# State-space x tiles of a hybrid diffusion layer turned to token-major by VectorE's 32x32 blocks and a pass through DRAM instead of by TensorE, with a group's B tile projected last

## The chip, the core and the metric

The kernel runs on one core of one Trainium2 chip. Five engines with a queue each work side by side: TensorE (PE in the profile; its weight loads are PEld), VectorE (DVE), ScalarE (ACT), GpSimd (POOL) and SyncE (SP), which here does little but issue transfers. The engines share the on-chip memory SBUF, the matmuls write to PSUM, and 16 DMA engines move data between DRAM and SBUF. Each engine takes its instructions in order; an instruction that waits holds up everything behind it on its engine. The metric is device time in microseconds (us), as the median over runs.

## What is computed

One layer over 512 latent tokens and 256 context tokens of width 1024, all in float32: a modulated RMSNorm, one wide input projection that feeds a bidirectional state-space mixer (Mamba-2 SSD, 4 groups of 8 heads) and a windowed attention, a gated merge, and a convolutional feed-forward part. The change touches how the state-space mixer gets its inputs. Cut to that:

```python
def ssd_prepare(xbc_raw, dt_raw, conv_w, conv_b, dt_bias, a_log):
    xbc = jax.nn.silu(dwconv_centred(xbc_raw, conv_w, conv_b))        # along tokens, per channel
    xs = xbc[..., :D_SSD].reshape(Bsz, L, SSD_GROUPS, SSD_HPG, SSD_HEADDIM)    # x: 2048 channels
    bm = xbc[..., D_SSD:D_SSD + D_BC].reshape(Bsz, L, SSD_GROUPS, SSD_STATE)   # B: 4 x 128
    cm = xbc[..., D_SSD + D_BC:].reshape(Bsz, L, SSD_GROUPS, SSD_STATE)        # C: 4 x 128
    ...
def ssd_scan(xs, la, bm, cm, h0, with_output):
    states = jnp.einsum('bcsgn,bgrcs,bcsgrp->bcgrpn', bc, decay_to_end, xc)    # sums over tokens s
    ...
    y_diag = jnp.einsum('bgrcls,bcsgrp->bclgrp', scores, xc)                   # sums over tokens s
    y_off = jnp.einsum('bclgn,bcgrpn,bgrcl->bclgrp', cc, states[:, :-1], jnp.exp(cs))
```

The convolution runs along tokens for each channel, so it wants channels on the partitions. The two sums over tokens `s` want x with tokens on the partitions. So every x tile is turned once between the two. The context tokens go through the same steps and give the scan its first states.

## The kernel before

**Products.** A float32 product is made of three fast passes: `split` (L182) makes of each weight tile (128 x 1024, `wraw`) a high part `whi` on ScalarE (L183, a cast) and a low part `wlo` on VectorE (L184, a subtraction), and `gemm` (L231) adds high x high, high x low and low x high in PSUM (L237, L238, L240). A latent product (LAT, 512 tokens wide) is 24 matmuls, a context product (CTX, 256 wide) is 24 shorter ones. The weight stream is loaded by SyncE into three `wraw` buffers; `whi` and `wlo` have two each. `run` (L210) issues load and split of the next step's weights ahead of each step.

**Projection steps.** `proj_steps(g)` (L1422) makes the six steps of a head group g: a B tile (`b_fn`, LAT and CTX), a C tile (`c_fn`, LAT) and four x tiles (`x_fn`, LAT and CTX). Each product goes through `conv_silu` (L1394): a ScalarE pass from PSUM (L1390), two VectorE passes (L1391, L1392), a tanh on ScalarE (L1398) and a last VectorE pass (L1399) that writes the channel-major tile, `tc` for x.

**Turning.** The finished tile is put on the list `TURN`; `turn` (L1413) makes a 128x128 TensorE transpose of each block of it into a PSUM bank (L1418: four for latent, two for context) and ScalarE copies the bank to its place in `xs` or `xsc` (L1462; L1439 for B). The transposes are emitted between the matmuls of a later product, by the list `BETWEEN`, which `gemm` calls at every third k.

**Scan.** `ssd_steps(g)` (L1486) scans group g while the projections of group g+1 run. Its first part, `states`, weighs the context tiles (`xw<-xsc`, L1491), multiplies them with the context B tiles (L1520) and walks back over the chunks (L1503). Then for each chunk of 128 tokens `chunk_in` builds the decay tiles `E` (L1593 to L1602) and `chunk_out` multiplies the states with C (L1610), the x tile with `E` (L1618) and turns the result (L1631).

**Order.** The loop at L1654 strings these together: after group 0's six steps comes, for each g, the `states` step, one filler product ("filler" below: a z or a gate tile, LAT alone), then the six steps of the next group with one chunk of group g behind each from the second on; for the last group fillers stand in place of projections. Within that, the scheduler of the tile framework fixes the order of each engine's queue before the program runs, from its own estimate of when things are ready. `xsc` has one buffer, `xs`, `BT`, `Bk` two, PSUM's `acc` three and `mis` five.

Of the kernel before, what the change touches and what calls it, by code (L numbers as in the profile page):

```python
# [9 lines left out]
F32 = mybir.dt.float32  # L10
# [8 lines left out]
P = 128  # L19
D = 1024  # L20
L = 512
LC = 256
# [22 lines left out]
def tile_hybrid_layer(  # L45
# [31 lines left out]
    nc = tc.nc  # L77
    V, S, G, T = nc.vector, nc.scalar, nc.gpsimd, nc.tensor
# [28 lines left out]
    def accb():  # L107
        return bank("acc")
# [158 lines left out]
    dt_d = dpool.tile([64, L + LC], F32, name="dt_d")  # L267
    tt_d = dpool.tile([64, 4], F32, name="tt_d")
    x1_d = dpool.tile([L, D], F32, name="x1_d")
    g2_d = dpool.tile([D], F32, name="g2_d")  # L270

    def col(base, i):
# [1121 lines left out]
    def conv_silu(ps, n, i, o):  # L1394
        a = tmp("ta")
        conv_half(ps, n, V_CW, V_CB, i, 24, a)
        t = tmp("tb")
        S.activation(t[:, :n], a[:, :n], AF.Tanh)  # L1398
        V.scalar_tensor_tensor(o[:, :n], t[:, :n], 1.0, a[:, :n], ALU.add, ALU.mult)  # L1399
# [13 lines left out]
    def turn(n=None):  # L1413

        for t, n_, put in TURN[:n]:
            ps = misb()
            for c in range(n_):
                T.transpose(ps[:, c * P : (c + 1) * P], t[:, c * P : (c + 1) * P], ident)  # L1418
            put(ps)
        del TURN[:n]  # L1420

    def proj_steps(g):  # L1422
        d = GR[g]

        def b_fn(w):
            d["xs"] = bp.tile([P, 4, 512], F32, tag="xs", name="xs", bufs=2)
            d["xsc"] = bp.tile([P, 2, 512], F32, tag="xsc", name="xsc", bufs=1)
            d["Bkc"] = bp.tile([P, 2, P], F32, tag="Bkc", name="Bkc", bufs=2)
            d["Bk"] = bp.tile([P, 4, P], F32, tag="Bk", name="Bk", bufs=2)
            d["BT"] = bp.tile([P, L], F32, tag="BT", name="BT", bufs=2)  # L1430
            pl, pc = accb(), accb()
            gemm([LAT(pl)], w)
            turn()
            gemm([CTX(pc)], w)
            conv_silu(pl, L, 16 + g, d["BT"])
            BTc = tmp("tc")
            conv_silu(pc, LC, 16 + g, BTc)
            for t, n, k in ((d["BT"], 4, d["Bk"]), (BTc, 2, d["Bkc"])):
                TURN.append((t, n, lambda ps, n=n, k=k: S.copy(flat(k), ps[:, : n * P])))  # L1439

        def c_fn(w):
            d["CT"] = bp.tile([P, L], F32, tag="CT", name="CT", bufs=2)
            pl = accb()
            gemm([LAT(pl)], w)
            turn(1)
            conv_silu(pl, L, 20 + g, d["CT"])

        def x_fn(ct, w):
            i = 4 * g + ct
            pl, pc = accb(), accb()  # L1450
            gemm([LAT(pl)], w)
            if not BETWEEN:
                BETWEEN.extend([lambda: None, lambda: turn(1), turn])
            gemm([CTX(pc)], w)
            for pp, n, dst in ((pl, L, d["xs"]), (pc, LC, d["xsc"])):
                xl = tmp("tc")
                conv_silu(pp, n, i, xl)
                TURN.append(
                    (
                        xl,  # L1460
                        n // P,
                        lambda ps, n=n, dst=dst: S.copy(  # L1462
                            dst[:, :, ct * P : (ct + 1) * P], ps[:, :n].rearrange("p (a b) -> p a b", b=P)
                        ),
                    )
                )
# [811 lines left out]
```

## Time and profile before

| | us |
|---|---|
| three runs: median (lowest to highest) | 1220.63 (1220.55 to 1221.63) |
| the profiled execution, its own time | 1221.22 |
| span of its instructions in the trace | 1219.4 |
| TensorE busy within the span | 1211.3 |
| VectorE / ScalarE / GpSimd busy | 924.5 / 684.4 / 182.3 |
| projections and scan, from the first group's first product to the last chunk | about 366 to 715 |

The profile lists, for each group of instructions, the source line, the engine, output<-input by the program's names, the shape and the count. A timeline row begins with the start in us from the span's start and the duration; what stands in brackets is idle time of the engine just before and who ended it. The starts of successive matmuls tell what each costs TensorE; the durations printed beside them overlap. The granted TensorE clock was 0.999 of full speed.

### The profile page before, as it was taken

How to read it: one execution, taken by the hardware profiler on the slowest of the kernel's cores; microseconds unless marked ns; L12 is line 12 of the kernel's file. 1: busy time of each engine (PE TensorE's matmuls, PEld its weight loads, DVE VectorE, ACT ScalarE, POOL GpSimd, SP SyncE). 2: the span in 40 equal slices, each digit the busy share in tenths (PEclk: the TensorE clock that was granted, in tenths of full speed). 3: DMA queues.
4: the chain of work that ended last, by engine and by line, in shares of the span. 5: the costliest groups of instructions: out<-in, count | busy, mean ns of one | idle time of the engine just before them, and what ended most of it. 6: DMA issues, size and time to landing. Idle time of an engine off the chain costs nothing.

```text
span 1219.4 us, 17443 instructions
## 1 busy us (share of the span) xinstructions
PE 1211.3 (99%) x6320; PEld 995.9 (82%) x6320; DVE 924.5 (76%) x1491; ACT 684.4 (56%) x1271; POOL 182.3 (15%) x183
## 2 busy tenths in 40 slices
PE   9999999999999999999999999999999999999997
PEld 6798888888878877778787778888988888888886
DVE  5857888888564698697896867677687877778778
ACT  5657787788544457476575664223544343436653
POOL 0000121100000043262451632000200000000021
PEclk9999999999999999999999999999999999999999
DMA  9645889844756335357366568777265534336662
GB/s 368 260 138 184 160 242 260 171 149 126 176 160 162 111 117 164 128 125 203 97 159 204 155 209 281 217 248 240 51 162 147 179 115 139 112 122 228 194 182 96
DMA packets 121383, 211.55 MB, mean 173 GB/s; under 512 B 25672, under 2 KB 67728, under 8 KB 121296
## 3 DMA queue, kind: packets, MB, share of 16 engines
q1 hardware_dynamic: 110256, 187.09, 49.4%
q0 software_dynamic: 10752, 23.07, 8.5%
q8 instruction: 50, 0.82, 0.3%
q14 instruction: 37, 0.30, 0.1%
q10 hardware_dynamic: 288, 0.27, 0.1%
HBM read 185.68 MB, written 42.28 MB: 187 GB/s over the span
## 4 chain that ended last, share of the span: by engine, by line
PE 96%; DVE 1%; issue 1%; ACT 1%; DMA 1%; POOL 0%; SPq 0%; POOLq 0%; DVEq 0%; ACTq 0%
PE acc L237 20%; PE acc L240 20%; PE acc L238 20%; PE score L957 3%; PE po L1006 3%; PE pt L993 2%; PE mis L579 2%; PE mis L1610 2%; PE mis L1503 2%; PE mis L1618 1%; PE mis L2137 1%; PE mis L2138 1%; PE mis L2139 1%; PE acc L2137 1%; PE acc L2139 1%; PE acc L2138 1%
## 5 line engine op out<-in xcount | busy, mean ns | idle before, releaser
L183 ACT CAST whi<-wraw 128x1024 fp32r<-128x1024 f32 (+1 forms) x115 | 120.6, 1049 | 158.0 <-PE acc L238 109.5
L184 DVE TENSOR_TENSOR wlo<-wraw,whi 128x1024 fp32r<-128x1024 f32 (+1 forms) x115 | 144.6, 1258 | 68.7 <-ACT whi L183 65.0
L237 PE MATMUL acc<-hlh,whi 128*128 128x512 f32 x472 | 194.2, 411 | 0.0
L238 PE MATMUL acc<-hll,whi 128*128 128x512 f32 x472 | 185.0, 392 | 0.0
L240 PE MATMUL acc<-hlh,wlo 128*128 128x512 f32 x472 | 184.9, 392 | 0.0
L237 PE MATMUL acc<-mh,whi 128*128 128x512 f32 x368 | 143.6, 390 | 0.0
L238 PE MATMUL acc<-ml,whi 128*128 128x512 f32 x368 | 143.2, 389 | 0.0
L240 PE MATMUL acc<-mh,wlo 128*128 128x512 f32 x368 | 143.2, 389 | 0.0
L240 PEld LDWEIGHTS acc<-hlh,wlo 128*128 128x128 f32 x472 | 88.6, 188 | 19.5
L237 PEld LDWEIGHTS acc<-hlh,whi 128*128 128x128 f32 x472 | 88.8, 188 | 17.9 <-issue 3.1
L238 PEld LDWEIGHTS acc<-hll,whi 128*128 128x128 f32 x472 | 88.9, 188 | 17.4 <-issue 2.4
L237 PEld LDWEIGHTS acc<-mh,whi 128*128 128x128 f32 x368 | 69.1, 188 | 14.5
L238 PEld LDWEIGHTS acc<-ml,whi 128*128 128x128 f32 x368 | 69.1, 188 | 14.3
L240 PEld LDWEIGHTS acc<-mh,wlo 128*128 128x128 f32 x368 | 69.1, 188 | 14.2
L1391 DVE SCALAR_TENSOR_TENSOR ta<-acc,half,ta 128x511 f32<-128x511 f32 (+1 forms) x66 | 43.9, 666 | 26.3 <-ACT ta L1390 26.0
L966 DVE CUSTOM_DVE_ANT_0 p<-score,winm,nsink 128x512 f32<-128x512 f32 (+1 forms) x64 | 51.9, 811 | 15.3 <-PE score L957 13.8
L1390 ACT ACTIVATE ta<-acc,half 128x512 f32<-128x512 f32 (+1 forms) x66 | 46.9, 710 | 22.1 <-PE acc L240 20.8
L973 ACT ACTIVATE p<-p,mneg 128x512 f32<-128x512 f32 (+1 forms) x64 | 49.8, 778 | 15.4 <-DVE mneg L966 14.8
L237 PE MATMUL acc<-hch,whi 128*128 128x256 f32 x176 | 54.7, 311 | 0.0
L1505 POOL TENSOR_TENSOR st<-st,eT 128x512 f32<-128x512 f32 x24 | 29.8, 1243 | 165.3 <-ACT st L1522 151.9
L164 POOL DMA_DIRECT2D dsum<-wdn x24 | 25.4, 1144 | 193.0 <-DVE wlo L1090 171.7
L795 DVE SCALAR_TENSOR_TENSOR tm<-wraw,csil,tm 128x512 f32<-128x512 f32 x56 | 44.1, 787 | 13.1 <-DMA wraw<-wm 12.5
(440 smaller groups left out, 2998.2 us busy)
## 6 DMA issues: line engine op xcount, KB each, us to landing
wraw<-wup SPq DMA_DIRECT2D x44, 512.0 KB, 3.7
dsum<-wdn POOLq DMA_DIRECT2D x24, 704.0 KB, 8.5
fb<-cs_d SPq DMA_DIRECT2D x32, 512.0 KB, 6.5
wraw<-wm SPq DMA_DIRECT2D x32, 512.0 KB, 3.9
wraw<-wx SPq DMA_DIRECT2D x24, 512.0 KB, 3.5
wm<-wm SPq DMA_DIRECT2D x16, 512.0 KB, 8.1
wraw<-wz SPq DMA_DIRECT2D x16, 512.0 KB, 3.9
wraw<-wos SPq DMA_DIRECT2D x16, 512.0 KB, 4.8
```

The lines of the kernel that those rows point to most:

```text
L183: F["cast"] = S.copy(hi[:, :n], r[:, :n])
L184: return V.tensor_tensor(lo[:, :n], r[:, :n], raw(hi[:, :n]), ALU.subtract)
L237: T.matmul(ps, wh, xh[:, k0 + k, :], start=a, stop=False)
L238: T.matmul(ps, wh, xl[:, k0 + k, :], start=False, stop=False)
L240: T.matmul(ps, wl, xh[:, k0 + k, :], start=False, stop=b)
L795: V.scalar_tensor_tensor(acc, r[:, u * 512 : u * 512 + 512], sc, acc, ALU.mult, ALU.add)
L957: T.matmul(ps[:, o : o + len(z) * P], Q[h][:, b * P : (b + 1) * P], k[:, j, z[0] * P : (z[-1] + 1) * P], start=v == 0 and o % 512 in (0, P ...
L966: V.tensor_tensor_reduce(p[:, :w], d["ps"][i][:, o0 : o0 + w], m, op0=ALU.add, op1=ALU.min, scale=1.0, scalar=nsink[:, h : h + 1], accum_o ...
L973: S.activation(p, p, AF.Exp, bias=d["mneg"][:, i : i + 1], scale=-1.0, accum_out=d["den"][:, i : i + 1])
L1006: T.matmul(d["po"], vst[:, cols[x], j, :], d[y][x], start=x == 0 and y == "pth", stop=x == c - 1 and y == "ptl")
L1390: S.activation(o[:, :n], ps[:, :n], AF.Identity, scale=hcol(base_w, stride + i), bias=hcol(base_b, i))
L1391: V.scalar_tensor_tensor(o[:, 1:n], ps[:, 0 : n - 1], hcol(base_w, i), o[:, 1:n], ALU.mult, ALU.add)
```

## The change

All four groups are in `BY_BLOCKS`. For them an x tile is no longer turned by TensorE and copied by ScalarE. `blocks_out` turns the 32x32 blocks of the channel-major tile in place on VectorE (`V.transpose`, one for the latent and one for the context tile) into `xb`, which lies in the one-buffer tiles `q2` and `rbc4`, and writes it to a DRAM tile `xs_d` with four transfers each, in runs of 32 floats (128 bytes), so that the blocks come to lie token-major. `blocks_in`, called in the next step, reads the channel columns back into `xs` and `xsc` in runs of 512 bytes, one transfer each. All of these are on SyncE's queue, which also carries the weights. The six steps of a group now run x0, C, x1, x2, x3, B. The B tile is still turned by TensorE.

```diff
+    xs_d = [dpool.tile([L + LC, 512], F32, name="xs_d%d" % g) for g in range(4)]
...
+    BY_BLOCKS = (0, 1, 2, 3)
+
+    def blocks_out(g, ct, n0, n, x):
+
+        t = hpool.tile([P, L], F32, tag="q2" if n == L else "rbc4", name="xb")[:, :n]
+        V.transpose(t, x[:, :n])
+        for a in range(4):
+            c = ct * P + 32 * a
+            o = xs_d[g][n0 : n0 + n, c : c + 32].rearrange("(f i) j -> i f j", i=32)
+            nc.sync.dma_start(o, t[32 * a : 32 * a + 32, :].rearrange("i (f j) -> i f j", j=32))
+
+    def blocks_in(g):
+
+        for ct in READY:
+            c = slice(ct * P, (ct + 1) * P)
+            for x, n0, n in ((GR[g]["xsc"], L, LC), (GR[g]["xs"], 0, L)):
+                nc.sync.dma_start(x[:, :, c], xs_d[g][n0 : n0 + n, c].rearrange("(a p) c -> p a c", p=P))
+        del READY[:]
...
         def b_fn(w):
...
             gemm([LAT(pl)], w)
             turn()
+            blocks_in(g)
             gemm([CTX(pc)], w)
...
         def c_fn(w):
...
+            blocks_in(g)
             gemm([LAT(pl)], w)
...
         def x_fn(ct, w):
             i = 4 * g + ct
             pl, pc = accb(), accb()
+            if blocks and not ct:
+                x_tiles()
+            blocks_in(g)
             gemm([LAT(pl)], w)
-            if not BETWEEN:
+            if not BETWEEN and not blocks:
                 BETWEEN.extend([lambda: None, lambda: turn(1), turn])
             gemm([CTX(pc)], w)
             for pp, n, dst in ((pl, L, d["xs"]), (pc, LC, d["xsc"])):
                 xl = tmp("tc")
                 conv_silu(pp, n, i, xl)
+                if blocks:
+                    blocks_out(g, ct, 0 if n == L else L, n, xl)
+                    continue
                 TURN.append(
...
+            if blocks:
+                READY.append(ct)
...
-        return r
+        return [r[2], r[1], *r[3:], r[0]] if blocks else r
```

Line numbers of the changed kernel are one higher than before up to the new functions and 37 higher behind them. Three places show how it moves instructions.

**The end of the first group's projections.** `tc_4389` is the context tile of x3 after its convolution, `acc_4412` the latent product of the B tile, `acc_4485` the filler, `acc_4531` the next group's first product with its weight halves `whi_4481` and `wlo_4482`. VectorE before (here `acc_4383` is x3's product, `acc_4465` the filler and `wlo_4462` the weights of the product behind it):

```order
L1391 TENSOR_SCALAR ta_4444<-acc_4383,half_90,ta_4444 128x511
L1392 TENSOR_SCALAR ta_4444<-acc_4383,half_90,ta_4444 128x511
L1399 TENSOR_SCALAR tc_4443<-tb_4448,ta_4444 128x512
L184 TENSOR_TENSOR wlo_4462<-wraw_4459,whi_4461 128x1024
L1391 TENSOR_SCALAR ta_4452<-acc_4384,half_90,ta_4452 128x255
L1392 TENSOR_SCALAR ta_4452<-acc_4384,half_90,ta_4452 128x255
L1399 TENSOR_SCALAR tc_4451<-tb_4456,ta_4452 128x256
L1491 TENSOR_TENSOR xw_4500<-xsc_4023,TD_3662 128x512
L1491 TENSOR_TENSOR xw_4502<-xsc_4023,TD_3662 128x512
```

VectorE now:

```order
L1400 TENSOR_SCALAR tc_4389<-tb_4394,ta_4390 128x256
L1428 STREAM_TRANSPOSE xb_4383<-tc_4375 128x512
L1392 TENSOR_SCALAR ta_4464<-acc_4412,half_90,ta_4464 128x511
L1393 TENSOR_SCALAR ta_4464<-acc_4412,half_90,ta_4464 128x511
L1428 STREAM_TRANSPOSE xb_4397<-tc_4389 128x256
L1400 TENSOR_SCALAR BT_4411<-tb_4468,ta_4464 128x512
L1392 TENSOR_SCALAR ta_4472<-acc_4413,half_90,ta_4472 128x255
L1393 TENSOR_SCALAR ta_4472<-acc_4413,half_90,ta_4472 128x255
L1400 TENSOR_SCALAR tc_4471<-tb_4476,ta_4472 128x256
L766 TENSOR_SCALAR te_4526<-tb_4524,acc_4485 128x512
L1528 TENSOR_TENSOR xw_4520<-xsc_4029,TD_3666 128x512
L184 TENSOR_TENSOR wlo_4482<-wraw_4479,whi_4481 128x1024
```

The context transpose `xb_4397` stands behind two passes over the B product, and the low half of the next weights stands behind the first reader of `xsc`. SyncE's queue at the same place, now (before, the loads of the B step, the filler and the next product followed one another with nothing between them):

```order
L1432 DMA xs_d0_104<-xb_4383 32x16x32 x3
L1432 DMA xs_d0_104<-xb_4397 32x8x32 x4
L1439 DMA xs_4028<-xs_d0_104 128x4x128
L177 DMA wraw_4479<-wx 128x1024
L1439 DMA xsc_4029<-xs_d0_104 128x2x128
L767 DMA zs_d_97<-te_4526 128x512
```

The weights `wraw_4479` are loaded behind the four context writes, and the read of `xsc` behind that load. On TensorE the next product now begins with two matmuls, then the product of the weighed context, and only then the first use of the low half:

```order
L237 MATMUL acc_4531<-hlh_109,whi_4481 128x512
L238 MATMUL acc_4531<-hll_110,whi_4481 128x512
L1557 MATMUL mis_4541<-xw_4520,Bkc_4409 128x512
L240 MATMUL acc_4531<-hlh_109,wlo_4482 128x512
L237 MATMUL acc_4531<-hlh_109,whi_4481 128x512
```

**The first chunk of the second group's scan**, VectorE before, up to the tiles `E` that TensorE waits for (`mis_5437` is the chunk's product of C and B):

```order
L184 TENSOR_TENSOR wlo_5486<-wraw_5483,whi_5485 128x1024
L1391 TENSOR_SCALAR ta_5426<-acc_5334,half_90,ta_5426 128x255
L1392 TENSOR_SCALAR ta_5426<-acc_5334,half_90,ta_5426 128x255
L1597 COPY_PREDICATED E_5444<-sel_85,mis_5445 128x512
L1399 TENSOR_SCALAR tc_5425<-tb_5430,ta_5426 128x256
L1597 COPY_PREDICATED E_5455<-sel_85,mis_5456 128x512
L1602 TENSOR_TENSOR E_5444<-E_5444,mis_5437 128x512
L1602 TENSOR_TENSOR E_5455<-E_5455,mis_5437 128x512
```

VectorE now:

```order
L1428 STREAM_TRANSPOSE xb_5459<-tc_5451 128x512
L1392 TENSOR_SCALAR ta_5466<-acc_5365,half_90,ta_5466 128x255
L184 TENSOR_TENSOR wlo_5532<-wraw_5529,whi_5531 128x1024
L1393 TENSOR_SCALAR ta_5466<-acc_5365,half_90,ta_5466 128x255
L1634 COPY_PREDICATED E_5490<-sel_85,mis_5491 128x512
L1400 TENSOR_SCALAR tc_5465<-tb_5470,ta_5466 128x256
L1634 COPY_PREDICATED E_5501<-sel_85,mis_5502 128x512
L1428 STREAM_TRANSPOSE xb_5473<-tc_5465 128x256
L1639 TENSOR_TENSOR E_5490<-E_5490,mis_5483 128x512
L1649 TENSOR_TENSOR te_5572<-mis_5570,TU_3665 128x512
L1639 TENSOR_TENSOR E_5501<-E_5501,mis_5483 128x512
```

Two transposes of the next group's x0, and a pass of the chunk's output (`te_5572`), have come in ahead of the last write of `E`. Further up in the same stretch a second `wlo` has come in and two `xw` passes have gone behind the chunk.

**The end of the last group's projections**, TensorE before (`acc_6946` is the filler behind the last projection):

```order
L1418 MATMUL mis_6916<-ident_79,tc_6820 128x128 x2
L237 MATMUL acc_6946<-hlh_105,whi_6851 128x512
L238 MATMUL acc_6946<-hll_106,whi_6851 128x512
L240 MATMUL acc_6946<-hlh_105,wlo_6852 128x512
L237 MATMUL acc_6946<-hlh_105,whi_6851 128x512
L238 MATMUL acc_6946<-hll_106,whi_6851 128x512
L240 MATMUL acc_6946<-hlh_105,wlo_6852 128x512
L1418 MATMUL mis_6953<-ident_79,tc_6920 128x128 x4
```

TensorE now (`BT_6931` and `tc_6996` are the latent and the context B tile, `acc_6933` the context product of B, `acc_7014` the filler):

```order
L240 MATMUL acc_6933<-hch_111,wlo_6814 128x256
L1419 MATMUL mis_7021<-ident_79,BT_6931 128x128 x4
L1419 MATMUL mis_7036<-ident_79,tc_6996 128x128 x2
L237 MATMUL acc_7014<-hlh_109,whi_6925 128x512
L238 MATMUL acc_7014<-hll_110,whi_6925 128x512
L240 MATMUL acc_7014<-hlh_109,wlo_6926 128x512
```

Both turns of the B tile stand ahead of the filler instead of between its matmuls. The filler's weights are loaded behind the context writes of the last x tile, and its `wlo` stands on VectorE right behind the pass that makes `tc_6996`.

More of the change, by code (lines that the diff above doesn't have):

```diff
@@ L1420, in turn, with x_tiles, b_fn @@
         del TURN[:n]
+    BY_BLOCKS = (0, 1, 2, 3)
[12 more added lines that the diff above has]
+        del READY[:]
+    READY = []
     def proj_steps(g):
         d = GR[g]
-        def b_fn(w):
+        blocks = g in BY_BLOCKS
+        def x_tiles():
             d["xs"] = bp.tile([P, 4, 512], F32, tag="xs", name="xs", bufs=2)
             d["xsc"] = bp.tile([P, 2, 512], F32, tag="xsc", name="xsc", bufs=1)
+        def b_fn(w):
+            if not blocks:
+                x_tiles()
             d["Bkc"] = bp.tile([P, 2, P], F32, tag="Bkc", name="Bkc", bufs=2)
@@ L1450, in x_fn @@
             pl, pc = accb(), accb()
+            if blocks and not ct:
+                x_tiles()
+            blocks_in(g)
             gemm([LAT(pl)], w)
-            if not BETWEEN:
+            if not BETWEEN and not blocks:
                 BETWEEN.extend([lambda: None, lambda: turn(1), turn])
```

## The prediction

> **What bounds the kernel now.** I read the busy times first, then the chain of waits, then the busy time by windows over the stretch with the projections and the scan (start:end and length in us, then PE, PEld, DVE, ACT and POOL busy with counts, the granted clock, the DMA share, GB/s).
>
> ```profile
> PE 1211.3 (99%) x6320; PEld 995.9 (82%) x6320; DVE 924.5 (76%) x1491; ACT 684.4 (56%) x1271; POOL 182.3 (15%) x183
> PE 96%; DVE 1%; issue 1%; ACT 1%; DMA 1%; POOL 0%; SPq 0%; POOLq 0%; DVEq 0%; ACTq 0%
> 440.00:500.00 60.00, 60.00 (x360) 47.61 (x359) 50.01 (x77) 40.73 (x99) 21.59 (x22) 1.00 0.58 167
> 500.00:560.00 60.00, 60.00 (x327) 45.84 (x327) 53.65 (x80) 40.10 (x96) 28.06 (x26) 1.00 0.47 127
> 560.00:620.00 60.00, 60.00 (x329) 45.87 (x328) 46.46 (x70) 34.20 (x75) 22.18 (x19) 1.00 0.44 128
> ```
>
> TensorE sets the time: 96% of the chain, and no gap in the windows. So every TensorE instruction taken out is worth its full cost, unless something that TensorE waits for comes later. ScalarE has a third of its time free, VectorE in one window only 60 − 53.65 = 6.35 us of 60, a tenth.
>
> **What is removed.** The turns on TensorE and the copies on ScalarE (engine, operation, count, then shortest/median/longest in ns and first and last start), and the starts on TensorE around one context product that carries six turns:
>
> ```profile
> L1418 PE MATMUL mis<-ident,tc x104: 270/272/331, 387.4 to 657.6; 128*128 128x128 f32 x104
> L1462 ACT COPY xs<-mis x16: 564/569/588, 396.6 to 655.4; 128x512 f32<-128x512 f32 x16
> L1462 ACT COPY xsc<-mis x16: 359/373/376, 398.5 to 657.9; 128x256 f32<-128x256 f32 x16
> 395.94 0.60 PE L1418 MATMUL mis<-ident,tc 128*128 128x128 f32 x4
> 396.50 0.28 PE L238 MATMUL acc<-hcl,whi 128*128 128x256 f32 x1
> 396.62 0.28 PE L240 MATMUL acc<-hch,wlo 128*128 128x256 f32 x1
> 397.45 0.38 PE L1418 MATMUL mis<-ident,tc 128*128 128x128 f32 x2
> 397.90 0.40 PE L238 MATMUL acc<-hll,whi 128*128 128x512 f32 x1
> 398.13 0.39 PE L240 MATMUL acc<-hlh,wlo 128*128 128x512 f32 x1
> 402.90 0.39 PE L240 MATMUL acc<-hlh,wlo 128*128 128x512 f32 x1
> ```
>
> The 104 hold 8 turns of B's context tiles, which stay; 96 go. What they cost must come from starts, since durations of pipelined matmuls overlap. Context matmuls follow each other by 396.62 − 396.50 = 0.12 us, latent ones by (402.90 − 398.13)/21 = 0.227 (21 matmuls lie between the two rows). From the four turns to the second matmul behind them is 0.56 us, of which one matmul is 0.12: the four cost 0.44. From the two turns likewise 397.90 − 397.45 − 0.23 = 0.22. Together 0.66 us for an x tile, and for 16 tiles **−10.56 us**. The 16 × (0.569 + 0.373) = 15.1 us of ScalarE's copies were beside TensorE's work and free nothing on the path.
>
> **What is added in steady state.** The same way through 32x32 blocks and DRAM is already gone in the kernel's last part, by `te` and `x_d` (for transfers: count, KB each, median us from issue to landing; "DMA to landing" gives least, median and most for L1959).
>
> ```profile
> L1956 DVE STREAM_TRANSPOSE te<-x x8: 699/706/707, 865.1 to 926.2; 128x512 f32<-128x512 f32 x8
> L1959 SPq DMA_DIRECT2D x_d<-te x32: 303/480/1637, 865.9 to 940.9; - x32
> DMA to landing us min/median/max: 1.7/3.7/4.8
> zs_d<-te SPq DMA_DIRECT2D x16, 256.0 KB, 2.6
> q<-tc SPq DMA_DIRECT2D x16, 128.0 KB, 2.7
> xt<-x_d SPq DMA_DIRECT2D x4, 512.0 KB, 5.9
> wraw<-wx SPq DMA_DIRECT2D x24, 512.0 KB, 3.5
> ```
>
> VectorE gains 0.706 us for the latent tile and about half, 0.35, for the context one: 1.06 a tile, 17 us in all. A step with LAT and CTX is 24 × 0.227 + 24 × 0.12 = 5.46 + 2.88 = 8.34 us on TensorE. At the idle share of the fullest window VectorE has 0.9 us free in it, elsewhere 1.4 (50.01) to 1.9 (46.46). So the transposes just fit on average, and I cost them only at the points where TensorE waits for VectorE. SP gains 10 issues a tile, 10 × 0.48 = 4.8 us in a step of 8.34, and a read there waits up to 3.7 us for its writes, which holds up the weights behind it. Since those have three buffers and land in 3.5 us, a load may be a step late: I take 0 for that in mid-group. A tile is 384 KB each way, less than one weight tile of 512, and the DMA share is 0.44 to 0.58: 0 too.
>
> The Trainium skill, "VectorE: DVE Perf Modes", section "Rules for kernel authors", would do a 128x128 transpose on TensorE where PSUM may be the destination, and speaks against the change. No run here shows the two beside each other; by that rule, were all of VectorE's 17 us on the path against 10.56 saved, the time would rise by some 6 us.
>
> **Boundary behind group 0.** Here the tile that is needed soonest comes last. Before:
>
> ```profile
> 365.85 0.39 PE L237 MATMUL acc<-hlh,whi 128*128 128x512 f32 x1
> 415.68 0.69 DVE L1399 SCALAR_TENSOR_TENSOR tc<-tb,ta 128x512 f32<-128x512 f32 x1 [1.03 <-ACT tb L1398]
> 416.75 0.58 ACT L1390 ACTIVATE ta<-acc,half 128x256 f32<-128x256 f32 x1
> 419.31 0.42 DVE L1399 SCALAR_TENSOR_TENSOR tc<-tb,ta 128x256 f32<-128x256 f32 x1 [0.55 <-ACT tb L1398]
> 420.67 1.29 DVE L1491 TENSOR_TENSOR xw<-xsc,TD 128x512 f32<-128x512 f32 x2 [0.94 <-ACT xsc L1462]
> 421.92 0.39 PE L237 MATMUL acc<-hlh,whi 128*128 128x512 f32 x1
> 422.98 1.23 DVE L184 TENSOR_TENSOR wlo<-wraw,whi 128x1024 fp32r<-128x1024 f32 x1 [1.01 <-ACT whi L183]
> ```
>
> TensorE starts the group at 365.85. Without x turns five steps of 8.34 and C's 5.46 put the end of B's LAT at 410.13, of its CTX at 413.01, of the filler (5.46 and B's turns, 0.66) at 419.13. On VectorE x3's context transpose stands behind two passes over B's latent product. In the rows x3's own context passes take until about 2.98 us behind their first ScalarE pass (416.75 to 419.73); two latent passes behind an accumulation take about 2.55 in the new place, which gives 412.68, and the transpose ends at 413.03. Four writes follow at 0.48, the last issued 414.47, landing 3.7 later at 418.2. The read of `xsc` is 128 KB: between 2.7 and 5.9 us by the two rows of loads; I take 4.0, nearer to `q`, which has its size. It lands at 422.2. Then one `xw` (half of 1.29) and `wlo` (1.23): the low half is there at 424.1. TensorE needs it after two matmuls (0.45) and one product of the weighed context (0.9, half of what L1610's two products take in the rows below, 521.51 to 523.32) from 419.13, so at 420.5: it waits **+3.6 us**. Least: with the transfers at no cost, the loading of the weights themselves (issued behind the writes at about 415.8, 3.5 us, then cast 1.05 and `xw`, `wlo`) gives 422.2, +1.8. Most: writes 4.8 and read 5.9 give 3.0 more, +6.6.
>
> **Boundaries behind groups 1 and 2.** The same, but a chunk of the scan lies between, on TensorE from the first row below to the last:
>
> ```profile
> 521.51 1.88 PE L1610 MATMUL mis<-st,CT 128*128 128x512 f32 x4
> 521.56 1.50 DVE L1602 TENSOR_TENSOR E<-E,mis 128x512 f32<-128x512 f32 x2
> 523.32 1.09 PE L1618 MATMUL mis<-E,xs 128*64 128x128 f32 x16
> 523.71 0.68 DVE L1612 TENSOR_TENSOR te<-mis,TU 128x512 f32<-128x512 f32 x1
> 525.45 0.47 PE L237 MATMUL acc<-hlh,whi 128*128 128x512 f32 x1
> ```
>
> That is 3.94 us of cover against 3.6: nothing by the median rows, **+0.5** for both since the cover is that thin; 0 at least, and with the slowest landings 6.6 − 3.94 = 2.7 each, +5.4.
>
> **First chunk of each scan (groups 0 to 2).** In these rows the last `E` is ready at 523.06, 0.26 us ahead of the L1618 that reads it: no reserve. Ahead of it VectorE gains two transposes (1.06) and one more `wlo` (1.23), loses two `xw` (1.29), and has `te` (0.68) between the two writes of `E`: 1.68 net. With the 0.9 us that VectorE idles in a step, 0.8 reaches TensorE, three times: **+2.4**. Bounds: 0 if all fits into idle time; 1.68 + 0.66 (TensorE arrives earlier by its missing turns) each, +7.
>
> **End of the last group's projections.** TensorE now takes B's context turn before the filler and has nothing else to do. `tc` of B is ready 2.98 us after CTX and a drain of 0.2; B's four latent turns cover some 0.2 of it: **+3.0**. Least 1.7 (passes back to back, under the latent turns), most 4 (the `wlo` behind it, 1.23, less the filler's first two matmuls).
>
> **Sum.** −10.56 + 3.6 + 0.5 + 2.4 + 3.0 = −1.06 us on the profiled execution's 1221.22: 1220.16. The median, 1220.63, lies 0.59 below that execution: **1219.6 us**. All low ends give −10.56 + 1.8 + 1.7 = −7.1, so 1213.6; all high ends −10.56 + 6.6 + 5.4 + 7 + 4 = +12.4, so 1233.1.
>
> **Rivals.**
> - *The stalls stay at their floor (faster).* Transfers land at their least (1.7, 2.7), and VectorE fits the rest into its idle time. Then 1.8 stays behind group 0, 2.0 at the last group, 0.8 at one first chunk: −10.56 + 4.6 = −6.0, 1214.7. For it speaks that the DMA engines are half idle; against, that `E` has no reserve and that the last turn waits whatever the transfers do.
> - *The transfers crowd out (slower).* The writes in 128-byte runs keep the DMA engines long enough that each boundary sees the slowest landings, 4.8 and 5.9: 3.0 more behind group 0, 5.4 in place of 0.5 behind groups 1 and 2, the last group's stall covering its own: 1219.6 + 7.9 = 1227.5. It decides once writes and read together take over 3.7 + 4.0 + 0.34 = 8.0 us, from where the chunk (3.94 against 3.6) no longer covers them. Against it: `x_d<-te`, with the same runs, takes 3.7 where `zs_d<-te` takes 2.6 for its 256 KB; for it, 5.9 for the load from `x_d`.
>
> The Trainium skill, "DMA: Bandwidth & Descriptors", section "Specifications", asks for 512 bytes or more for line rate and has shorter writes done as read-modify-write. Here 128-byte runs are read against 3.7 and 2.6 us, which fits a penalty that hides behind a fixed cost; by that rule at full strength this rival would be the forecast.
>
> - *VectorE becomes the bound (slower).* A group with its four chunks takes 5 × 8.34 + 2 × 5.46 + 4 × 3.94 = 68.4 us of TensorE, in which VectorE gains 4 × 1.06 = 4.2, or 3.7 in 60: the fullest window goes from 53.65 to 57.4, 96%, and an in-order engine that waits for inputs may not reach that. If one group pays its four tiles in full, +4.2: 1223.8. It decides where VectorE idles less than a transpose in a step. Against: the idle time of the other windows.
>
> That the turns would not leave TensorE at all is ruled out by its order of instructions.
>
> **Chances.** Forecast 0.40 (its own range 1217 to 1222.5), floor 0.22, crowded transfers 0.23, VectorE 0.15. The range 1213.5 to 1228 leaves out the worst sums. A change under 0.2% (2.4 us, 1218.2 to 1223.0) cannot be told from none. The forecast gives 0.10 faster and 0.30 same; the floor is faster; crowding and VectorE are slower but for 0.02, and the forecast's tail adds a little: faster 0.32, same 0.28, slower 0.40.
>
> **What would show it.** Right: 24 turns left at L1419; busy windows of TensorE but for gaps ahead of the product at L1557 near 420 (3 to 4 us), ahead of L1655 in the first chunk of three groups (below 1 us each), and about 3 us ahead of the last group's filler; landings of the `xs_d` writes near 3.7. Wrong: gaps at `whi` or `wlo` in mid-group whose releaser is the weights' load (SP held up), landings of 5 us and more, a gap at every chunk, or no gap at the two ends of groups.

## The result and the profile after

The change made the kernel slower: 1236.0 us as the median of 4 runs (1234.57 to 1237.13) against 1220.68 (1220.55 to 1221.63), a ratio of 1.0123 with a 95% interval of 1.0108 to 1.0138. The forecast was 1219.6, the range 1213.5 to 1228: the time lies outside it, on the side that the forecast did not take. The profiled execution took 1234.57 us, 13.35 more than the one before.

The page of the changed kernel, busy times and the chain of waits:

```profile
PE 1209.6 (98%) x6224; PEld 987.5 (80%) x6224; DVE 937.4 (76%) x1523; ACT 670.9 (54%) x1239; POOL 185.6 (15%) x183
PE 89%; DVE 3%; DMA 2%; ACT 1%; issue 1%; SPq 1%; POOL 1%; POOLq 0%; DVEq 0%; ACTq 0%
```

TensorE has 96 instructions fewer, as it should, but its share of the chain fell from 96% to 89%: it now waits. The turn of a chunk's result (`dx`), which TensorE does four times in each group at a fixed place in the scan, shows where. Rows of the timeline for the first and the last chunk of group 0 and the first chunk of groups 1, 2 and 3, before:

```profile
453.73 0.60 PE L1631 MATMUL mis<-ident,dx 128*128 128x128 f32 x4
492.58 0.60 PE L1631 MATMUL mis<-ident,dx 128*128 128x128 f32 x4
532.79 0.60 PE L1631 MATMUL mis<-ident,dx 128*128 128x128 f32 x4
612.29 0.60 PE L1631 MATMUL mis<-ident,dx 128*128 128x128 f32 x4
686.29 0.60 PE L1631 MATMUL mis<-ident,dx 128*128 128x128 f32 x4
```

and after:

```profile
457.56 0.60 PE L1668 MATMUL mis<-ident,dx 128*128 128x128 f32 x4
494.90 0.60 PE L1668 MATMUL mis<-ident,dx 128*128 128x128 f32 x4
536.49 0.60 PE L1668 MATMUL mis<-ident,dx 128*128 128x128 f32 x4
618.95 0.60 PE L1668 MATMUL mis<-ident,dx 128*128 128x128 f32 x4
699.26 0.66 PE L1668 MATMUL mis<-ident,dx 128*128 128x128 f32 x4 [0.63 <-POOL dx L1660]
```

After minus before is 3.83, 2.32, 3.70, 6.66 and 12.97 us. Between the first and the last chunk of group 0 the change gains 1.51 us, about what the missing turns promise. Everything is lost ahead of group 0's first chunk and between the last chunk of one group and the first of the next. TensorE's waits from 340 to 760 us (what waited, for what, us in total, times, longest), of the changed kernel:

```profile
PE acc L237 <- ACT whi L183: 4.8, 4, 1.6
PE mis L1540 <- DVE xw L1528: 3.7, 2, 2.3
PE acc L240 <- DVE wlo L184: 1.8, 3, 0.7
PE mis L1419 <- DVE tc L1400: 1.5, 1, 1.5
PE mis L1557 <- DVE xw L1528: 1.4, 1, 1.4
```

Before, this view has no row at all. With three waits of 0.6 the sum is 15.0 us, and its largest part, 6.6, is for weights. The 5.1 us for `xw` go back to late loads as well. VectorE and ScalarE take their work in order, and what makes `xw` stands behind a pass whose load is late (the first row at the end of group 0, the second at the end of group 2), changed kernel:

```profile
425.56 1.37 DVE L794 TENSOR_SCALAR tm<-wraw,csil 128x512 f32<-128x512 f32 x1 [2.19 <-DMA wraw<-wm]
590.36 1.86 ACT L1630 ACTIVATE E<-fb,TX 128x128 f32<-128x128 f32 x6 [4.44 <-DMA fb<-cs_d]
```

The loads are late because SyncE sends them late and they land late. SyncE's waits before, and of the changed kernel:

```profile
SPq L177 <- DVE wlo L184: 171.5, 34, 10.6
```

```profile
SPq L1432 <- DVE xb L1428: 76.5, 20, 8.5
SPq L177 <- DVE wlo L184: 6.0, 6, 2.3
```

Before, SyncE spent 171.5 us waiting for a weight buffer to come free: each load left at the first moment it could. Now it stands 76.5 us at the writes of `xs_d`, waiting for transposes, and that row is down to 6.0. Whoever ended them, its waits ahead of weight loads (L177) come to some 41 us where they were 208: it is behind. At the end of group 1's projections this looks so (start, duration, what was issued), before:

```profile
496.94 0.33 SPq L177 DMA_DIRECT2D wraw<-wx  x1
502.54 0.32 SPq L776 DMA_DIRECT2D ts_d<-tb  x1
503.30 0.33 SPq L177 DMA_DIRECT2D wraw<-wm  x1
509.01 10.51 SPq L177 DMA_DIRECT2D wraw<-wx  x2
```

and in the changed kernel:

```profile
498.65 0.97 SPq L1681 DMA_DIRECT2D yz_d<-zs  x2
499.67 0.46 SPq L177 DMA_DIRECT2D wraw<-wm  x1
503.51 0.32 SPq L777 DMA_DIRECT2D ts_d<-tb  x1
504.35 3.29 SPq L1590 DMA_DIRECT2D zs<-zs_d  x4
507.69 1.64 SPq L177 DMA_DIRECT2D wraw<-wx  x2
509.38 3.98 SPq L1611 DMA_DIRECT2D fb<-cs_d  x2
513.46 3.24 SPq L177 DMA_DIRECT2D wraw<-wx  x1
```

Gate tiles (`zs`), decay tiles (`fb`) and three weight tiles go out in one burst behind the filler's store at 503.51, and the issues themselves get longer (3.24 us for one). The landing shows it (count, KB each, median us), changed kernel:

```profile
wraw<-wx SPq DMA_DIRECT2D x20, 512.0 KB, 7.4
fb<-cs_d SPq DMA_DIRECT2D x31, 512.0 KB, 8.9
xs_d<-xb SPq DMA_DIRECT2D x64, 64.0 KB, 2.2
xsc<-xs_d SPq DMA_DIRECT2D x16, 128.0 KB, 3.6
```

The weights take 7.4 us where they took 3.5. The new transfers themselves are quick. A load is slow where much is in flight ahead of it. Counted from the traces from 366 to 735 us, the median weight load found no other transfer in flight when it was issued before the change, and finds 1280 KB now. Of the changed kernel's, the nine that find under 600 KB land in 3.9 us, the 18 that find 1200 or more in 7.7.

Each longer wait also costs behind itself. The end of group 2 on TensorE, changed kernel:

```profile
600.93 0.72 PE L240 MATMUL acc<-hlh,wlo 128*128 128x512 f32 x1 [0.53 <-DVE wlo L184]
601.44 0.63 PE L237 MATMUL acc<-hlh,whi 128*128 128x512 f32 x1
601.86 0.63 PE L238 MATMUL acc<-hll,whi 128*128 128x512 f32 x1
...
604.68 0.39 PE L240 MATMUL acc<-hlh,wlo 128*128 128x512 f32 x1
```

Matmuls that follow one another by 0.23 us elsewhere take 0.42 here for some 3.5 us. The granted clock of the windows 601.04 to 604.45 and 662.48 to 665.89 is 0.50, and it is full elsewhere in this part: two stretches of 3.41 us, which cost about 1.7 us each. The Trainium skill, "TensorE: Matmul & The Clock Gate", section "Part 1: The HAM clock gate", has the array at half clock after an idle window of about 3.4 us, until it was busy that long again. The length and the half speed agree; but there was no idle stretch of 3.4 us. The 3.41 us ahead of 601.04 held waits of 1.20 and 0.53, those ahead of 662.48 held 2.86 us of waits, and the longest single wait of the part, 2.25 us up to 434.68, brought no half clock.

The account: 10.56 us of turns removed, 15.0 of waits, 3.4 of slower clock make +7.8; the profiled executions differ by 13.35. Part of the other 5.5 us are the edges of the waits. Around the wait of 1.62 us for `whi`, the matmul ahead is 0.39 long where its followers start 0.23 apart, and the one behind it takes 0.33: 0.26 us more than the row says, by which estimate the 14 waits have some 3.6. The rest was not taken apart.

### The profile page after: what moved, and what is told of

Same layout as the page of the kernel before. It is cut to its first block, busy times and chain, and to the rows that moved or that the text cites. A ratio compares the mean times of both kernels' runs of the same rounds, so it can differ in the third digit from the quotient of the medians.

```text
span 1232.8 us, 17467 instructions
## 1 busy us (share of the span) xinstructions
PE 1209.6 (98%) x6224; PEld 987.5 (80%) x6224; DVE 937.4 (76%) x1523; ACT 670.9 (54%) x1239; POOL 185.6 (15%) x183
## 4 chain that ended last, share of the span: by engine, by line
PE 89%; DVE 3%; DMA 2%; ACT 1%; issue 1%; SPq 1%; POOL 1%; POOLq 0%; DVEq 0%; ACTq 0%
PE acc L237 19%; PE acc L240 19%; PE acc L238 19%; PE score L958 3%; PE po L1007 3%; PE pt L994 2%; PE mis L580 2%; PE mis L1647 2%; PE mis L1540 1%; PE mis L2176 1%; PE mis L2174 1%; PE mis L2175 1%; PE acc L2176 1%; PE acc L2174 1%; PE acc L2175 1%
## 5 line engine op out<-in xcount | busy, mean ns | idle before, releaser
L184 DVE TENSOR_TENSOR wlo<-wraw,whi 128x1024 fp32r<-128x1024 f32 (+1 forms) x115 | 149.1, 1296 | 71.5 <-ACT whi L183 70.7
L237 PEld LDWEIGHTS acc<-hlh,whi 128*128 128x128 f32 x472 | 89.6, 190 | 23.9 <-ACT whi L183 5.8
L1002 DVE TENSOR_TENSOR ptl<-pt,pth 128x512 fp32r<-128x512 f32 x72 | 47.5, 685 | 8.5 <-ACT pth L998 7.7
```

The source lines that it names most:

```text
L184: return V.tensor_tensor(lo[:, :n], r[:, :n], raw(hi[:, :n]), ALU.subtract)
L237: T.matmul(ps, wh, xh[:, k0 + k, :], start=a, stop=False)
L1002: V.tensor_tensor(d["ptl"][x], d["pt"][x], raw(d["pth"][x]), ALU.subtract)
```

## The experiments

Medians in us, and ratios to the kernel before with 95% intervals. Most are the changed kernel with one edit more; x tiles are chosen by a set `BLK` of (group, tile) in place of `BY_BLOCKS`, the order by `LAST`, and `states` calls `blocks_in` too, which does nothing where B is last. e2, e5, e9 to e12 and e18 leave a part of the turn out, so the x that the scan reads is not the layer's; they serve for the time alone.

| run | x tiles turned by | writes issued by | median | ratio (interval) |
|---|---|---|---|---|
| e1 | TensorE, new order | none | 1221.39 | 1.0003 (0.9994 to 1.0013) |
| e5 | nothing, new order | none | 1213.65 | 0.9938 (0.9923 to 0.9953) |
| e2 | VectorE, no transfers | none | 1224.94 | 1.0037 (1.0024 to 1.0051) |
| e4 | blocks, order of before | SyncE | 1255.26 | 1.0282 (1.0265 to 1.0299) |
| e12 | ScalarE copies, transfers | SyncE | 1237.51 | 1.0133 (1.0118 to 1.0149) |
| e3 | blocks | GpSimd | 1226.31 | 1.0041 (1.0028 to 1.0055) |
| e18 | ScalarE copies, transfers | GpSimd | 1218.59 | 0.9979 (0.9970 to 0.9988) |
| e8 | blocks, weights by ScalarE | SyncE | 1238.81 | 1.0145 (1.0130 to 1.0160) |
| e13 | blocks, filler stores by ScalarE | SyncE | 1231.28 | 1.0089 (1.0073 to 1.0104) |
| e14 | blocks | ScalarE | 1267.55 | 1.0379 (1.0360 to 1.0398) |
| e16 | as e13 | GpSimd | 1225.69 | 1.0038 (1.0026 to 1.0051) |
| e10 | VectorE, x2 and x3 alone, no transfers | none | 1224.30 | 1.0030 (1.0018 to 1.0042) |
| e11 | VectorE, x0 and x1 alone, no transfers | none | 1215.83 | 0.9959 (0.9944 to 0.9973) |
| e9 | as e2, B turned later | none | 1226.05 | 1.0048 (1.0031 to 1.0065) |
| e6 | blocks x0 to x2, TensorE x3 | GpSimd | 1230.99 | 1.0088 (1.0071 to 1.0105) |
| e15 | blocks x0, x1, order of before | GpSimd | 1229.04 | 1.0064 (1.0049 to 1.0079) |
| e7 | blocks x0 to x2 of group 0, order of before | GpSimd | 1221.24 | 1.0000 (0.9991 to 1.0010) |
| e17 | blocks x0, x1 of group 0, order of before | GpSimd | 1220.24 | 0.9993 (0.9984 to 1.0002) |

### The parts of the change, one at a time

e1 keeps only the order:

```diff
-    BY_BLOCKS = (0, 1, 2, 3)
+    BLK = ()
+    LAST = True
...
-        return [r[2], r[1], *r[3:], r[0]] if blocks else r
+        return [r[2], r[1], *r[3:], r[0]] if last else r
```

> All x tiles turned by TensorE as before, only the order of the six steps is the new one (x0, C, x1, x2, x3, B). If the order is what costs (B's tile and its turns come last), it shows here: 1228 us or more. If SyncE's queue, VectorE or the DMA engines cost, this stays within 3 us of before: 1220 to 1224, with the turn of B's context tile ahead of the last filler as its one gap (about 3 us).

1221.39: the order alone costs nothing that can be measured. e5 then takes the turns away altogether and fills `xs` and `xsc` with a constant:

```diff
+            for n in ("xs", "xsc"):
+                G.memset(d[n], 0.5)
...
-                    blocks_out(g, ct, 0 if n == L else L, n, xl)
                     continue
...
-            if blocks:
-                READY.append(ct)
```

> x is turned nowhere: no TensorE turn, no copy, no transpose on VectorE, no transfer; GpSimd fills xs and xsc with a constant, so x is wrong behind it. Order of the steps as in the change. This measures the term removed by itself. If the turns cost TensorE 0.66 us a tile, 10.56 us less than the run with the new order alone (1221.4): 1210.8, 1210 to 1212. If part of the turns lay in time that TensorE has anyway, or if the B turn now waits whatever VectorE does, more: 1213 to 1217. The distance to the run without transfers (1224.9) is then what the transposes on VectorE cost.

1213.65, so the turns are worth 7.7 us against e1, not 10.56. A scan step with its x tile takes 12.8 us instead of 13.5, so the 0.66 a tile is right; 2.8 us come back: 1.6 as small waits (1.01 for VectorE's pass on a modulation tile, 0.3 twice for B's context tile), the rest was not taken apart. By the turns of `dx`, from the first chunk of one group to that of the next e5 gains 2.1, 1.3 and 1.1 us on e1, where four tiles promise 2.64.

e2 adds VectorE's transposes, without transfers:

```diff
-        t = hpool.tile([P, L], F32, tag="q2" if n == L else "rbc4", name="xb")[:, :n]
-        V.transpose(t, x[:, :n])
-        for a in range(4):
...
+        d = GR[g]["xs" if n == L else "xsc"][:, :, ct * P : (ct + 1) * P]
+        V.transpose(d, x[:, :n].rearrange("p (a b) -> p a b", b=P))
```

> The transposes of 32x32 blocks stay on VectorE but write straight into xs and xsc, and no transfer of xs_d is left: the blocks are not put in their places, so x is wrong behind it. VectorE, TensorE and the order are those of the change. If VectorE's 17 us cost, it stays at 1230 to 1236. If the transfers cost, through SyncE's queue or through the DMA engines, it comes to 10.56 us saved less about 3 for the last turn and 0 to 2 for the first chunks: 1212 to 1216.

Neither: 1224.94, 11.3 us above e5. VectorE at the end of group 0's scan in e5:

```profile
489.88 0.69 DVE L1400 SCALAR_TENSOR_TENSOR BT<-tb,ta 128x512 f32<-128x512 f32 x1 [0.17 <-ACT tb L1399]
```

and in e2, where TensorE then waits 1.67 us for this tile:

```profile
488.16 0.45 DVE L1429 STREAM_TRANSPOSE xsc<-tc 128x256 f32<-128x256 f32 x1
488.64 1.29 DVE L1522 TENSOR_TENSOR xw<-xsc,TD 128x512 f32<-128x512 f32 x2
492.14 0.69 DVE L1400 SCALAR_TENSOR_TENSOR BT<-tb,ta 128x512 f32<-128x512 f32 x1 [0.16 <-ACT tb L1399]
```

x3's context transpose, and two `xw` that it makes ready, have come ahead of B's passes. B is last and has no reserve, so TensorE waits. In e2 TensorE's three waits for B's latent tile come to 5.9 us.

e12 is the other half: the transfers with VectorE relieved. ScalarE copies the tiles, so SyncE still waits for an engine at each write.

```diff
-        V.transpose(t, x[:, :n])
+        S.copy(t, x[:, :n])
```

> All transfers of the change, on SyncE, but ScalarE copies each x tile into xb in place of VectorE's transpose, so the blocks are not turned and x is wrong; VectorE has the work of the run that turns x nowhere. If the transfers cost their 11 us by themselves (held weights), it comes to 1213.7 + 11 = 1225, with whi waits of TensorE as in the change (4.8 us). If they cost only because VectorE's transposes are late and SyncE waits for them, 1214 to 1218. If transfers and transposes cost together and not in sum, 1230 or more.

1237.51, no better than the change: the last of its cases. With the transfers on SyncE the whole loss is there without one transpose on VectorE: the two costs, 11.3 and 23.9 above e5, do not add up (the change is at +22.3); the transfers cover the other. SyncE stands 65.2 us at the writes for ScalarE's copies. So what is shown is that the writes cost as much behind another engine; no run has writes on SyncE that wait for nothing. TensorE's waits for weights in e12:

```profile
PE acc L237 <- ACT whi L183: 6.0, 5, 1.7
PE acc L240 <- DVE wlo L184: 3.4, 5, 0.9
```

e4 puts back only the order of before (`LAST = False`).

> All x tiles by blocks and DRAM as in the change, but the order of before (B, C, x0 to x3). If the order costs, this is 1215 to 1224. If SyncE's queue or the DMA engines cost, it is as slow as the change or slower, since x3 then has no step between its writes and its use: 1233 to 1245.

1255.26, above its bracket: without B's step between x3 and its use, one wait for `whi` alone is 12.5 us. So the order belongs to the blocks, and does not cost by itself.

### Which queue, and what on it

e3 changes the engine that issues the writes:

```diff
-            nc.sync.dma_start(o, t[32 * a : 32 * a + 32, :].rearrange("i (f j) -> i f j", j=32))
+            G.dma_start(o, t[32 * a : 32 * a + 32, :].rearrange("i (f j) -> i f j", j=32))
```

> The 128 writes of xs_d are issued by GpSimd instead of SyncE; the bytes, the runs of 128 bytes and the reads stay. If SyncE's queue costs (its in-order waits for the transposes hold up the weights), the waits at the writes go with them and most of the loss comes back: 1214 to 1222, the weights landing near 3.5 us again. If the DMA engines are crowded, or VectorE is the bound, it stays at 1231 to 1238.

1226.31, between the two cases: 9.7 of the 15.3 us come back. Landing in e3:

```profile
wraw<-wx SPq DMA_DIRECT2D x20, 512.0 KB, 3.9
xs_d<-xb POOLq DMA_DIRECT2D x64, 64.0 KB, 4.5
```

The same bytes move, and the weights land in 3.9 us, not 7.4; the median weight load finds 256 KB in flight and not 1280. One thing changes with the engine: from 366 to 735 us the changed kernel moves 53,678 packets under 512 bytes (before: 2,214), e3 only 4,679, as GpSimd's queue makes larger packets of the same writes. That the short packets are not what slows the weights is shown by e14 below, which moves 53,470 of them. The waits for weights are gone; those of e3 are

```profile
PE mis L1671 <- POOL dx L1663: 4.1, 3, 2.1
PE mis L1560 <- DVE xw L1530: 3.4, 4, 1.5
```

GpSimd's in-order queue now stands at the writes, and `dx`, which GpSimd computes, comes late. e18 joins e3 with ScalarE's copies:

> Writes by GpSimd as in the third run, and ScalarE's copies in place of VectorE's transposes, so x is wrong. With SyncE's queue free of the writes, VectorE's share can show: if the transposes cost what they cost without transfers (up to 11 us), 1215 to 1219; if what is left above 1213.7 is GpSimd's and the late reads, it stays at 1224 to 1228.

1218.59, at the upper end of the first case: 7.7 us below e3. It differs from e12 in the issuing engine alone: with copies in place of transposes the move to GpSimd's queue is worth 18.9 us. The waits for `dx` are gone. So here the transposes cost, and partly through the queue: GpSimd stands at a write until VectorE comes to the transpose.

e8 leaves the writes and moves the weights:

```diff
-        dma = nc.sync.dma_start(r[:, :n], a)
+        dma = (nc.scalar if key[0] in "xg" else nc.sync).dma_start(r[:, :n], a)
```

> The change with the loads of the projection and filler weights issued by ScalarE instead of SyncE; the 160 transfers of xs and their waits stay on SyncE. If weights held up behind those waits are what SyncE's queue costs, it comes to what moving the writes away gives, 1222 to 1228, the whi waits of TensorE gone. If the crowded DMA engines make them late, or other loads held up on SyncE (decay tiles, gates), or ScalarE is held up by its new issues, it stays at 1232 or more.

1238.81: no gain. The waits have moved, as e8's rows show:

```profile
PE mis L1542 <- DVE xw L1530: 7.6, 4, 3.1
PE mis L1560 <- DVE xw L1530: 3.6, 2, 2.1
```

`whi` is down to one wait of 0.5. It is not the weights as such: what stays on SyncE's queue, here x itself (`xsc` lands in 5.5 us, not 3.6) and other tiles, is late in their place. And a queue of their own does not make the weights land soon: they take 6.3 us, as SyncE's bursts still run beside them (832 KB in flight at the issue in the median). e13 takes the filler's stores off the queue (`nc.scalar` for the stores in `z_step` and `g_step`), behind which the burst above went out:

> The change, with the stores of the finished filler tiles (zs_d and ts_d) issued by ScalarE. In the change SyncE waits at these stores at the end of each group, and four gate tiles, decay tiles and two to three weight tiles go out in one burst behind them and take 7 to 10 us to land. If the hold at these stores is what makes them late, the burst goes out earlier: 1224 to 1231, fewer whi and wlo waits. If the writes and reads of xs themselves hold SyncE just as long, no gain: 1234 to 1238.

1231.28, just above the first case: 4.7 us come back. SyncE still stands 72.0 us at the writes for transposes. The stores are part of it, the writes the larger part. With both moved:

> All 16 tiles by blocks, new order, writes issued by GpSimd and filler stores by ScalarE. SyncE then waits for nothing but buffers and the landing of the writes. If what is left above the run that turns x nowhere (1226.3 against 1213.7) is SyncE's, 1218 to 1222; if it is the late transposes, B's passes and dx, no change: 1224 to 1229.

1225.69, no more than e3 alone. e14 has ScalarE issue the writes (`nc.scalar` for `nc.sync`):

> The 128 writes of xs_d issued by ScalarE (a third of its time is free) and not by SyncE; reads and bytes as in the change. If SyncE's queue is what costs, as with GpSimd: 1222 to 1230, weights landing in about 4 us. If waiting for transposes merely moves to ScalarE's queue and holds its passes (conv, whi), TensorE waits for whi and BT instead: 1230 or more.

1267.55, the worst of all. The weights land in 3.9 us again, with all the short packets, but ScalarE's passes stand behind the waiting writes (35.3 us of idle time ahead of the tanh at L1399 alone end with such a transfer), and what they feed is late:

```profile
PE mis L1658 <- DVE E L1642: 14.8, 5, 5.6
PE acc L237 <- DVE ta L1393: 11.2, 2, 6.2
```

### Where VectorE's part sits

e9 turns B later in the filler (`BETWEEN.extend([lambda: None, turn])` at L1569, from e2).

> The run without transfers (transposes straight into xs and xsc, x wrong; 1224.9), but B's two turns are both emitted at the second place in the filler, some nine matmuls (2 us) later. There TensorE waited 1.7 to 2.4 us for the latent B tile at the end of groups 1 to 3. If the transposes cost mainly by making B late for these turns, most of the 11.3 us above the run that turns x nowhere (1213.7) go: 1216 to 1219. If they cost by filling VectorE everywhere, the waits move to xw and E and it stays at 1222 or more.

1226.05, no gain, but the waits have not moved to `xw` and `E`: TensorE waits as long, 2.2 to 2.3 us each, for B's context tile. That tile is what ends last. e10 and e11 transpose half of the tiles:

> Without transfers, and only x2 and x3 of each group are transposed on VectorE (8.5 of its 17 us), x0 and x1 are filled by GpSimd, so x is wrong. If what is late at the group's end comes from the last tiles, nearly all of the 11.3 us stay: 1222 to 1225. If it goes by the amount of VectorE work, half: 1218 to 1220.

> The mirror: only x0 and x1 transposed, x2 and x3 filled. Last tiles to blame: 1213 to 1216. Amount to blame: 1218 to 1220. If the first chunk of each scan is the place, which x0's transposes precede, then this one is the slower of the two, 1220 to 1225.

1224.30 and 1215.83: 10.7 and 2.2 us above e5. Equal work, five times the cost: without transfers it is the place, not the amount.

### Can a part of the saving be kept?

e6 gives x3 back to TensorE, e15 x2 and x3 with the order of before; e7 and e17 keep blocks in group 0 alone, where no scan runs beside them.

> New order, writes issued by GpSimd, but x3 of each group turned by TensorE: 12 tiles by blocks, 7.9 us of turns saved. If the loss sits at the ends of the groups (x3's transposes ahead of B's passes on VectorE, xsc late for the first xw), those stalls go, and only 2 to 4 us for GpSimd's late dx stay: 1215 to 1219. If it grows with the number of tiles, three quarters of the loss of the run with all writes on GpSimd stay: 1224 to 1227.

> Only x0 and x1 of each group by blocks and DRAM (writes by GpSimd), x2 and x3 turned by TensorE, order of before. 8 x 0.66 = 5.3 us of turns go, nothing of xs is late at a group's end, and VectorE's half as many transposes cost 2.2 us by the run with x0 and x1 alone. If GpSimd's queue costs nothing: 1217 to 1218.5. If its late dx costs 1 to 2 us in each group, as in the runs with writes on GpSimd: 1220 to 1224.

> Blocks for x0, x1 and x2 of group 0 alone, where no scan runs beside them, writes issued by GpSimd, order of before (B first). Three turns, 3 x 0.66 = 2 us, go. If stalls come from what the blocks meet in the scan and at the group's end, nothing takes their place: 1218.5 to 1219.5. If the transposes or transfers cost wherever they are: 1221 to 1224.

> Only x0 and x1 of group 0 by blocks and DRAM, writes by GpSimd, order of before: two turns, 2 x 0.66 = 1.3 us, and both tiles are back long before the group's end, where the run with x0 to x2 lost 1.1 us on a late xw. If blocks are free where nothing is late: 1219.2 to 1219.8. If not: 1220.5 or more.

e6 at 1230.99 and e15 at 1229.04 miss both of their cases upward: each has fewer tiles by blocks than e3 and is slower. In e6 TensorE waits 4.0 us for `dx`, 2.8 for a pass on a gate tile and 1.9 for a tile to be turned; in e15 2.3 for `dx` and 5.6 for passes of VectorE that other work was put ahead of. In e15 the windows 540 to 600 and 600 to 660 have a granted clock of 0.97, some 1.7 us each; in e6 600 to 660 has it. Each such edit makes the scheduler lay out the queues anew, in e3 and e18 too, so these costs cannot be had by scaling the tiles; what else makes these two so much worse stays open. e7 gives nothing (one wait of 1.12 for `xw`, its context tile coming late), and e17, at 1220.24, between its cases, has no wait left but an interval that reaches over 1. No version that turns all of x was clearly faster than the kernel before.

## Why the prediction was wrong, point by point

- **The removal** (−10.56). Right for a tile, 0.66 us. As a term of the sum 7.7 was measured (e1 against e5): 2.8 us of it did not arrive, 1.6 of them lost to small waits.
- **SyncE's queue** ("a load may be a step late: I take 0 for that in mid-group", and 0 for the DMA share). This is the step that failed. I had the numbers, 4.8 us of issues in a step of 8.34 and reads that wait for writes, and looked at whether the three buffers would cover one late load. I did not ask where the queue stands while it waits for VectorE (76.5 us), nor what goes out when it is released: a burst in which weights land in 7.4 us. In mid-group the 0 held: a step of the scan takes 12.81 us, as in e5. At the groups' ends, where the sum has only the chain through x, late weights cost 6.6 us of waits and 5.1 more by way of `xw`. Taking the writes off the queue gives 9.7 us (e3) with the transposes on VectorE and 18.9 (e12 against e18) with copies on ScalarE.
- **The transposes** ("just fit on average", costed only at `E`). Wrong in size and place. At `E` TensorE waited 0.6 us once, where 2.4 were taken. They cost at the end of a group, where B, now last, had no reserve: 11.3 us without transfers, 7.7 with the writes on GpSimd (e3 against e18), and nothing visible behind SyncE's delay.
- **Behind group 0** (+3.6). 5.3 us of waits were measured: 1.6 for `whi`, then 1.4 and 2.3 for `xw`. The chain that I took, through the four writes and the read of `xsc`, was the wrong one: the writes landed in 1.7 to 2.2 us and the read in 3.6, below the 3.7 and 4.0 taken, and the weights came late. (`q<-tc`, taken there for a load, moves data within SBUF; its 2.7 us bore on the read of `xsc` only by its size.)
- **Behind groups 1 and 2** (+0.5). The chunk was to cover the transfers of x. It did, but the weights, gate and decay tiles behind them were not covered: 0.6 us for `wlo` at group 1's end, and 1.4 for `xw`, 1.2 and 0.5 for weights, and a stretch at half clock at group 2's.
- **The last group's end** (+3.0). 0.6 and 1.5 us for B's turns, 2.1 in all, near the 1.7 to 4 taken; 1.4 for `whi` behind them, a stretch at half clock from 662.48, 0.5 and 0.7 more for weights and 0.6 for `dx` were not foreseen.
- **The rivals.** Crowded transfers gave a slower time, 1227.5, but not by this way: the landings of x stayed short, and it was the weights, gate and decay tiles that landed late. The rule that short writes are slow, by the Trainium skill, "DMA: Bandwidth & Descriptors", section "Specifications", did not show as slow landings here: 64 KB in runs of 128 bytes landed in 2.2 us. The same bytes in longer runs were not timed. VectorE as the bound came out as a real cost with another place. The floor was wrong.
- **What was named as proof against the forecast**, gaps at `whi` and `wlo` behind late weights, is what the profile shows, though at the ends of the groups and not in mid-group.

## What to carry to other kernels

When transfers are added to a queue that also prefetches, first read how long that queue now waits for a free buffer: here 171.5 us of such waiting was the reserve that kept TensorE fed. A transfer that waits for a late engine turns this reserve into delay for everything behind it, and what is released together lands late together. Moving the waiting transfer to another engine's queue helps only as far as that engine has nothing urgent behind it, and a step that is put last makes every pass ahead of it on its engines part of the critical path.

## What the runs showed of the hardware

The Trainium skill, "DMA: Bandwidth & Descriptors", section "Issuing engines are not separate DMA queues", says that issuing from several engines saves only the sequencer's time to start a transfer. The 128 writes at a median of 0.45 us are some 58 us of SyncE's time, and the chain of waits has 1% of the span, some 12 us, for SyncE; moving them to GpSimd gave 9.7 us, and to ScalarE it cost 31.6, because of what stands behind a waiting transfer on each. A weight tile of 512 KB that found under 600 KB of other transfers in flight landed in a median of 3.9 us (the changed kernel), 3.7 (e3) and 4.2 (e8, from ScalarE's queue), and one that found 1200 KB or more in 7.7, 8.0 and 8.7. An issue on SyncE, 0.33 us for a weight tile before, took 3.24 in the burst above.

Waits of 1.20 and 0.53 us, close together, were followed by 3.41 us at half clock, which cost 1.7 more: a wait on TensorE can cost twice its length. Leaving out the first and last 15 us of each run, the clock in the traces has 27 stretches at half speed. Each is 3.41 us long or a multiple of it, and in the 3.41 us ahead of each TensorE stood idle for 1.60 us or more in all. Cut the time from 340 to 760 us of these runs into steps of 3.41 us that line up with such a stretch: of the steps with no half clock behind them, none had over 1.92 us idle. So here idle time of about half a step was enough, and it did not have to be one wait.
